# Hybrid DeltaNet and mLSTM layer: the step from 64-blocks to 128 in the inverse, all its products in pairs, with the last token block's matrices moved by transfers

## The chip, the cores and the metric

The kernel runs on one core of one Trainium2 chip. A core has five engines with instruction streams of their own: PE (TensorE, the matrix products), DVE (VectorE), ACT (ScalarE), POOL (GpSimd) and SP (SyncE, which here only issues transfers). Sixteen DMA engines carry the transfers that SP and ACT issue. The metric is the device time of one execution in microseconds.

## The reference

The layer takes 256 tokens of width 2048. From one wide projection of the normalized input come a gated DeltaNet with 32 value heads of 128 and an mLSTM with 8 heads; their outputs are projected, merged by gates and projected again. What the change touches is the DeltaNet's chunk algorithm, with chunks of 64 tokens:

```python
lower = jnp.where(strict, jnp.einsum('nbhid,nbhjd->nbhij', k_beta, kc) * decay, 0.0)
unit_lower = lower + jnp.eye(CHUNK, dtype=f32)
rhs = jnp.concatenate([v_beta, k_beta * jnp.exp(g_cum)[..., None]], axis=-1)
sol = lax.linalg.triangular_solve(unit_lower, rhs, left_side=True, lower=True, unit_diagonal=True)
...
def step(state, inp):
    attn_c, u_c, w_c, qd_c, kt_c, gt_c = inp
    v_new = u_c - jnp.einsum('bhck,bhkv->bhcv', w_c, state)
    o = jnp.einsum('bhck,bhkv->bhcv', qd_c, state) + jnp.einsum('bhij,bhjv->bhiv', attn_c, v_new)
```

The kernel doesn't carry a state from chunk to chunk. It treats 128 tokens as one block, inverts a unit triangular 128x128 matrix for each head and block, and applies it. The result is the same sequence.

## The kernel before

**The stream.** A planner (`Stream`) walks through all weight matrices in a fixed order. SP loads a piece of 1 MB into `raw` (line 169, a ring of three), ACT rounds it to `whi` (L173), DVE and at times POOL form the rest `wlo` (L174), and PE multiplies: projections with tokens on the output's rows are `pn` (L235), transposed ones are `pt` (L628 with `whi`, L632 with `wlo`). A piece is 1024 columns; PE does 12 products on it for `pn` and 16 pairs of high and low products for `pt`. The instruction order of each engine is the order in which the Python code calls it; no scheduler changes it.

**Side jobs.** After each used piece `side.step()` advances all side jobs, which are Python generators, by one `yield`. One step is thus one piece of projection work on PE. `wait(n)` lets n steps pass; `banks(n)` waits until n of the four PSUM slots for side jobs can be had; `side.debt` is an estimate of DVE time that other side jobs have yet to use, by which the block inverse on DVE is spread over steps (`side.room`).

**Periods.** The 32 heads are handled in eight periods, `zg` = 0 to 7, of two pairs each. In periods 0 to 5 the projection beside this work is mostly the DeltaNet's `pt`; in period 6 it is the mLSTM's `pn`, and in period 7 a `pt` of the mLSTM. A period has eight triangular 128x128 matrices: two blocks of 128 tokens for each of four heads, numbered m = 0 to 7; even m is a head's first 128 tokens, odd m its last. `au` holds the matrices, `um(m)` is the part of one that is inverted. The inverse grows from 32 to 64 to 128:

- `base_inverse` inverts the 32x32 diagonal blocks on DVE, in a packed form that SP moves through DRAM (`au` to `ud` to `ug`, then `xx` to `xd` to `xcmp`). `xcmp` and its transpose `ycmp` are copied to the diagonals of `x0` (128 rows, ACT) and `y0` (64 rows, DVE). `x0` becomes the inverse, `y0` the transpose of its first 64x64 block.
- `gdn_stage2` makes the off-diagonal 32x32 blocks with the products `mp` and `mx` and ACT's copies (L902 to `y0`, L905 to `x0`).
- The step from 64 to 128 needs, for every m, `mq` = the corner of `um(m)` times `y0` (first, L911: contracts rows 0 to 63, puts its output on rows 64 to 127) and `mz` = its copy `p2` times `x0` (second, L914: contracts rows 64 to 127, output on rows 0 to 63). As they use opposite corners of the array, an `mq` of one matrix and an `mz` of another can stand in a pair. Three blocks of instructions hold them: four `mq` of the even matrices; four `mq` of the odd ones with four `mz` of the even ones; and, behind the product `pa`, four `mz` of the odd ones.
- Then the inverse is applied: `pa` with the even inverses, `pb`, `pc` with the odd ones, and `po`.

**The waits around it.** `gdn_stage2` lets `wait(1 + (zg == 6))` steps pass between ACT's copies and the first `mq`, one step between the blocks, and two each ahead of `pb` and `pc`.

Of the kernel before, what the change touches and what calls it, by code (L numbers as in the profile page):

```python
# [7 lines left out]
F32 = mybir.dt.float32  # L8
F32R = mybir.dt.float32r
AF = mybir.ActivationFunctionType  # L10
# [5 lines left out]
P = 128  # L16
S = 256
# [101 lines left out]
def hybrid_layer_kernel(  # L119
# [25 lines left out]
    V, A, T, G, SP = nc.vector, nc.scalar, nc.tensor, nc.gpsimd, nc.sync  # L145
# [60 lines left out]
    def gtile(nm, held=False):  # L206
        i = slots[0] % 4
        slots[0] += 1
        t = pg.tile([P, 512], F32, name=nm, tag="g")
        freed[i] = 1 << 30 if held else side.t + 1  # L210
        slots[1][id(t)] = i, t
        return t

    def gfree(t):
        freed[slots[1].pop(id(t))[0]] = side.t

    def banks(n):

        while any(freed[(slots[0] + j) % 4] >= side.t for j in range(n)):
            yield  # L220
# [16 lines left out]
    side = Side()  # L237
    bp = x0 = y0 = None
# [209 lines left out]
    def branches_open():  # L448

        nonlocal bp, x0, y0  # L450
        side.drain()
        st.close()
        bp = br.enter_context(tc.tile_pool(name="bp", bufs=2))

        x0 = bp.tile([P, 8, P], F32, name="x0", tag="x0", bufs=1)
        y0 = bp.tile([64, 8, 64], F32, name="y0", tag="y0", bufs=1)
        G.memset(x0, 0.0)
        G.memset(y0, 0.0)

    def add_start_groups(bi):  # L460
# [12 lines left out]
        def after(g, ps):  # L473
            for b in range(2):
                if k0:
                    V.tensor_tensor(part[g][:, b], ps[b], part[g][:, b], op=ALU.add)  # L476
                elif bi or g in (0, 2, 3) or b == 0:
                    A.copy(part[g][:, b], ps[b])  # L478
                else:
                    V.tensor_copy(part[g][:, b], ps[b])  # L480
            if bi == len(BLOCKS) - 2 and g == 3:
                late_consts()
            if lastb:
                side.add(gate_values(g), 0)
                if g == NG - 1:
                    branches_open()
# [219 lines left out]
    def wait(n):  # L706
        for _ in range(n):
            yield
# [106 lines left out]
    def base_inverse(zg, res, zr):  # L815

        ud = res["ud"]
        xd = dr.tile([8, 4, 4, 8, 32], F32, name="xd", tag="xd", bufs=2)
        ug = bp.tile([P, 32, 32], F32, name="ug", tag="ug", bufs=1)
        for q in range(4):  # L820
            SP.dma_start(ug[32 * q:32 * q + 32],
                         ud[q].rearrange("m j i -> m (j i)").unsqueeze(0).broadcast_to([4, 8, 1024]))
        yield from wait(4)
        most = ROOM_US if zg else FIRST_ROOM_US
        yield from side.room(0.8, most)
        ugf = ug.rearrange("p j i -> p (j i)")
        V.memset(ugf[:, 0:1024:33], -1.0)
        nsu = bp.tile([P, 15], F32, name="nsu", tag="nsu", bufs=1)
        V.tensor_scalar(nsu, ugf[:, 34:34 + 66 * 15:66], -1.0, None, op0=ALU.mult)
        V.memset(ugf[:, 34:34 + 66 * 15:66], 0.0)  # L830
        xx = bp.tile([P, 8, 32], F32, name="xx", tag="xx", bufs=1)
        tmp = bp.tile([P, 8, 2, 32], F32, name="tmp", tag="tmp", bufs=1)
        V.tensor_copy(xx, eunit)
        for i in range(1, 32, 2):
            w = min(2, 32 - i)
            nq = (i + w - 2) // 4 + 1
            n = i + w
            us = 0.2 + 0.00105 * nq * w * n
            yield from side.room(us, most)
            V.tensor_tensor(tmp[:, 0:nq, 0:w, 0:n], xx[:, 0:nq, 0:n].unsqueeze(2).broadcast_to([P, nq, w, n]),  # L840
                            ug[:, 0:n, i:i + w].rearrange("p k c -> p c k").unsqueeze(1).broadcast_to([P, nq, w, n]),
                            op=ALU.mult)
            yield from side.room(us + 0.16 * (w - 1), most)
            V.tensor_reduce(xx[:, 0:nq, i:i + w], tmp[:, 0:nq, 0:w, 0:n], axis=AX.X, op=ALU.add, negate=True)
            if w == 2:
                V.scalar_tensor_tensor(xx[:, 0:nq, i + 1], xx[:, 0:nq, i], nsu[:, i // 2:i // 2 + 1],
                                       xx[:, 0:nq, i + 1], op0=ALU.mult, op1=ALU.add)
        yield from wait(1)
        SP.dma_start(xd.rearrange("qq q rg m i -> (q rg m) qq i"), xx)
        yield from wait(2 * (zg // 7))  # L850
        xcmp = bp.tile([P, 8, 32], F32, name="xcmp", tag="xcmp", bufs=1)
        for q in range(4):
            SP.dma_start(xcmp[32 * q:32 * q + 32], xd[:, q])
        yield from wait(5 - 2 * (zg // 7))
        side.debt += 1.1
        ycmp = bp.tile([P, 8, 32], F32, name="ycmp", tag="ycmp", bufs=1)
        V.transpose(ycmp.rearrange("p m i -> p (m i)"), xcmp.rearrange("p m i -> p (m i)"))
        for q in range(4):
            c = slice(32 * q, 32 * q + 32)
            A.copy(x0[c, :, c], xcmp[c])  # L860
            if q < 2:
                V.tensor_copy(y0[c, :, c], ycmp[c])
        res.update(xcmp=xcmp, ycmp=ycmp)
        yield
        while zg < 7 and side.t < res["t"] + STAGE2_STEPS - 1:
            yield
        side.add(gdn_stage2(zg, res, zr), 0)

    def gdn_stage2(zg, res, zr):

        au, xc, yc = [res["au", z] for z in range(2)], res["xcmp"], res["ycmp"]

        def um(m):
            return au[m // 4][:, m % 4 // 2, 256 + 384 * (m % 2):384 + 384 * (m % 2)]
# [8 lines left out]
        for m in range(8):  # L883
            for t in range(2):
                r, o = 64 * t, 64 * t + 32
                T.matmul(pss[t][o:o + 32, m * 32:(m + 1) * 32], um(m)[r:r + 32, o:o + 32], yc[r:r + 32, m],
                         start=True, stop=True)
        for t in range(2):
            o = 64 * t + 32
# [6 lines left out]
        for m in range(8):  # L896
            T.matmul(psx[0][32:64, S + m * 32:S + (m + 1) * 32], xc[32:64, m], pc_[32:64, m], start=True, stop=True)
            for t in (1, 0):
                r, o = 64 * t, 64 * t + 32
                T.matmul(psx[t][r:r + 32, m * 32:(m + 1) * 32], pc_[o:o + 32, m], xc[o:o + 32, m],  # L900
                         start=True, stop=True)
        A.activation(y0[32:64, :, 0:32], cols32(psx[0], S)[32:64], AF.Copy, scale=-1.0)  # L902
        for t in range(2):
            r = 64 * t
            A.activation(x0[r:r + 32, :, r + 32:r + 64], cols32(psx[t])[r:r + 32], AF.Copy, scale=-1.0)  # L905
            gfree(psx[t])
        yield from wait(1 + (zg == 6))
        p2 = bp.tile([P, 8, 64], F32, name="p2", tag="p2", bufs=1)

        def first(ps, j, m):  # L910
            T.matmul(ps[64:128, j * 64:(j + 1) * 64], um(m)[0:64, 64:128], y0[:, m], start=True, stop=True)  # L911

        def second(ps, j, m):
            T.matmul(ps[0:64, j * 64:(j + 1) * 64], p2[64:128, m], x0[64:128, m, 64:128], start=True, stop=True)  # L914

        def part64(ps, r, o):
            return ps[r:r + 64, o:o + S].rearrange("p (m i) -> p m i", m=4)

        yield from banks(1)
        psp = gtile("mq", True)  # L920
        side.debt -= 0.5
        for j in range(4):
            first(psp, j, 2 * j)
        A.activation(p2[64:128, 0:8:2], part64(psp, 64, 0), AF.Copy, scale=-1.0)
        yield
        yield from banks(1)
        psz = gtile("mz", True)
        side.debt -= 0.5
        for j in range(4):
            first(psp, 4 + j, 2 * j + 1)  # L930
            second(psz, j, 2 * j)
        A.copy(x0[0:64, 0:8:2, 64:128], part64(psz, 0, 0))
        A.activation(p2[64:128, 1:8:2], part64(psp, 64, S), AF.Copy, scale=-1.0)
        gfree(psp)
        yield

        rr = res["rr"].rearrange("p b z (h d) -> p b (z h d)", h=2)
# [1 line left out]
        heads = [(g, g // 2, g % 2, slice(g * P, (g + 1) * P)) for g in range(4)]  # L939
        yield from banks(1)  # L940
        pa = gtile("pa", True)
        side.debt -= 1.3
        for g, z, h, c in heads:
            T.matmul(pa[:, c], x0[:, 2 * g], rr[:, 0, c], start=True, stop=True)
        for j in range(4):
            second(psz, 4 + j, 2 * j + 1)
        A.copy(ys[:, 0], pa)
        gfree(pa)
        A.copy(x0[0:64, 1:8:2, 64:128], part64(psz, 0, S))
        gfree(psz)  # L950
        yield from wait(2)
        yield from banks(1)
        pb = gtile("pb", True)
# [42 lines left out]
        yield  # L996
        while "sz" not in zr:
            yield
        yield from wait(2)
        sz = zr["sz"]  # L1000
        for g, z, h, c in heads:
            if g == 2:
# [20 lines left out]
    def period_tail(zg, ps, qs, pr, res, zr):  # L1023
        yield from gdn_stage1(2 * zg + 1, ps, qs, pr, res)
        yield
        side.add(base_inverse(zg, res, zr), 2)
# [510 lines left out]
```

## Time and profile before

| | us |
|---|---|
| median of 3 runs | 1582.64 |
| lowest and highest run | 1582.38, 1582.78 |
| profiled execution, its own time | 1583.33 |
| its span, first to last instruction | 1581.6 |
| mean granted PE clock | 0.998 of full speed |

The profiled execution is 0.69 us above the median and 1.73 us longer than its span. In the page's rows a group stands as line, engine, operation, output<-input and count; `PE mq L911 x8` are eight passes of the four 64x64 products, since an f32 product shows two. All 64x64 products together are 256 passes:

```profile
L911 PE MATMUL mq<-y,au 64*64 64x64 f32 x128 | 10.8, 224 | 0.0
L914 PE MATMUL mz<-x,p 64*64 64x64 f32 x128 | 10.8, 224 | 0.0
```

The figures are busy time in us (passes that run side by side count once), mean ns of one, and idle time ahead of the group. A row of the chain of waits has a start, a length and what ran. A row of windows has the stretch, its length, the busy time and number of instructions of PE, PEld, DVE, ACT and POOL, the granted clock, the DMA engines' busy share and GB/s.

### The profile page before, as it was taken

Reading aid. Unit: us, or ns where it says so; the run is one execution under the profiler, and the core shown is the slowest. Engines: PE = TensorE matmul, PEld = TensorE weight load, DVE = VectorE, ACT = ScalarE, POOL = GpSimd, SP = SyncE. Lnnn points to the kernel's source line nnn. Section 1 sums busy time; section 2 is a strip of 40 time slices with the busy share of each in tenths; the row PEclk is TensorE's granted clock in tenths of the full one; section 3 lists DMA queues with packets and bytes.
Section 4 is the critical chain, followed back from the end, with each engine's and each line's share of the span. In section 5 each row is a group of like instructions: output and inputs, shape, how many; then the busy total and the mean of one; then the engine's idle time right before and its main releaser. Section 6 shows DMA issues by size and latency. Waiting matters only on the chain.

```text
span 1581.6 us, 23140 instructions
## 1 busy us (share of the span) xinstructions
PE 1565.7 (99%) x8574; PEld 1315.6 (83%) x8574; DVE 1159.7 (73%) x1884; ACT 967.2 (61%) x1608; POOL 249.7 (16%) x204
## 2 busy tenths in 40 slices
PE   8999999999999999999999999999999999999997
PEld 5888888888888888888888888888888888888886
DVE  6785556865789887988887988775868766756654
ACT  7754446765666676767676776766666554544443
POOL 4787761000000000000000000000000000100100
PEclk9999999999999999999999999999999999999999
DMA  9998775975565646575656565647878878766572
GB/s 379 392 385 334 267 288 188 288 245 193 182 195 175 209 147 202 167 201 168 202 167 198 172 199 171 199 142 247 281 270 314 339 264 298 282 237 237 213 269 107
DMA packets 167739, 372.22 MB, mean 235 GB/s; under 512 B 26021, under 2 KB 127797, under 8 KB 140105
## 3 DMA queue, kind: packets, MB, share of 16 engines
q1 hardware_dynamic: 167240, 370.13, 67.6%
q8 instruction: 67, 1.10, 0.3%
q10 hardware_dynamic: 290, 0.53, 0.1%
q14 instruction: 46, 0.38, 0.1%
q0 software_dynamic: 96, 0.09, 0.0%
HBM read 354.40 MB, written 16.31 MB: 234 GB/s over the span
## 4 chain that ended last, share of the span: by engine, by line
PE 81%; issue 13%; ACT 2%; DMA 1%; DVE 1%; POOL 1%; DVEq 0%; SPq 0%; ACTq 0%; POOLq 0%
PE pn L235 36%; PE pt L628 19%; PE pt L632 9%; PE py L235 8%; POOL mg L1327 1%; ACT whi L173 1%; DMA ya<-o_dr 1%; PE psa L235 1%; PE mq L911 1%; PE csil L305 0%; PE po L977 0%; PE pc L966 0%; PE po L976 0%; PE po L974 0%; PE pb L956 0%
## 5 line engine op out<-in xcount | busy, mean ns | idle before, releaser
L174 DVE TENSOR_TENSOR wlo<-raw,whi 128x1024 fp32r<-128x1024 f32 x453 | 556.1, 1235 | 241.1 <-ACT whi L173 240.2
L173 ACT CAST whi<-raw 128x1024 fp32r<-128x1024 f32 x516 | 532.1, 1046 | 261.3 <-PE pn L235 133.2
L235 PE MATMUL pn<-whi,h 128*128 128x512 f32 x1792 | 563.7, 392 | 0.9 <-ACT part L478 0.6
L628 PE MATMUL pt<-h,whi 128*128 128x512 f32 x1280 | 408.5, 400 | 0.0
L235 PEld LDWEIGHTS pn<-whi,h 128*128 128x128 f32 x1792 | 336.4, 188 | 71.9 <-ACT part L478 1.5
L235 PE MATMUL pn<-wlo,h 128*128 128x512 f32 x896 | 349.1, 390 | 0.9 <-POOL wlo L174 0.9
L632 PEld LDWEIGHTS pt<-h,wlo 128*128 128x128 f32 x1280 | 240.4, 188 | 56.6
L632 PE MATMUL pt<-h,wlo 128*128 128x256 f32 x1280 | 252.1, 278 | 0.0
L235 PEld LDWEIGHTS pn<-wlo,h 128*128 128x128 f32 x896 | 168.4, 188 | 35.4 <-POOL wlo L174 1.7
L628 PEld LDWEIGHTS pt<-h,whi 128*128 128x128 f32 x1280 | 195.4, 189 | 2.4
L174 POOL TENSOR_TENSOR wlo<-raw,whi 128x1024 fp32r<-128x1024 f32 (+1 forms) x63 | 145.7, 2320 | 51.6 <-ACT whi L173 51.6
L235 PE MATMUL py<-whi,yhi 128*128 128x512 f32 x384 | 150.8, 393 | 0.0
L235 PE MATMUL py<-whi,ylo 128*128 128x512 f32 x384 | 149.7, 390 | 0.0
L235 PE MATMUL py<-wlo,yhi 128*128 128x512 f32 x384 | 149.4, 389 | 0.0
L173 ACT CAST yhi<-ya 128x512 fp32r<-128x512 f32 x48 | 29.9, 622 | 130.3 <-PE py L235 114.9
L476 DVE TENSOR_TENSOR part<-pn,part 128x512 f32<-128x512 f32 x112 | 73.7, 685 | 45.2 <-PE pn L235 45.0
L719 POOL TENSOR_SCALAR_AFFINE_SELECT dd<-gb 128x256 f32<-128x256 f32 x40 | 25.9, 668 | 422.8 <-DMA gb<-rows 330.3
L174 DVE TENSOR_TENSOR ylo<-ya,yhi 128x512 fp32r<-128x512 f32 x48 | 33.2, 691 | 74.9 <-ACT yhi L173 72.2
L235 PEld LDWEIGHTS py<-whi,yhi 128*128 128x128 f32 x384 | 72.1, 188 | 15.6 <-ACT vt L1144 0.4
L235 PEld LDWEIGHTS py<-whi,ylo 128*128 128x128 f32 x384 | 72.1, 188 | 15.1
L235 PEld LDWEIGHTS py<-wlo,yhi 128*128 128x128 f32 x384 | 72.1, 188 | 14.9
L686 DVE SCALAR_TENSOR_TENSOR qs<-ab,gcv,qs 128x255 f32<-128x255 f32 (+2 forms) x192 | 81.0, 477 | 0.0
(263 smaller groups left out, 1612.9 us busy)
## 6 DMA issues: line engine op xcount, KB each, us to landing
raw<-in_dram SPq DMA_DIRECT2D x259, 1024.0 KB
ar<-in_dram SPq DMA_DIRECT2D x31, 1024.0 KB
raw<-in_dram SPq DMA_DIRECT2D x16, 512.0 KB
ya<-o_dr SPq DMA_DIRECT2D x32, 256.0 KB
gate_dr<-part SPq DMA_DIRECT2D x11, 512.0 KB
gb<-rows SPq DMA_DIRECT2D x20, 256.0 KB
raw<-in_dram SPq DMA_DIRECT2D x6, 768.0 KB
ug<-ud SPq DMA_DIRECT2D x32, 128.0 KB
```

The costliest lines, as they stand in the source:

```text
L173: A.copy(hi, src)
L174: (eng or V).tensor_tensor(lo, src, hi.bitcast(F32), op=ALU.subtract)
L235: T.matmul(ps, l, r, start=start and i == 0, stop=stop and i == 2, skip_group_check=True)
L476: V.tensor_tensor(part[g][:, b], ps[b], part[g][:, b], op=ALU.add)
L628: T.matmul(ps, hi[:, o:o + P], h2[:, k].rearrange("p a s -> p (a s)"), start=k == 0, stop=k == KC - 1, skip_group_check=True)
L632: T.matmul(ps[:, 0:S], lo[:, o:o + P], h_hi[:, k], start=False, stop=k == KC - 1, skip_group_check=True)
L686: V.scalar_tensor_tensor(dst[:, n, sh:], ab[i][:, 0:S - sh], taps(n, 3 - sh), dst[:, n, sh:], op0=ALU.mult, op1=ALU.add)
L719: G.affine_select(dd[:, :, blk * S:blk * S + P], gb[:, :, blk * P:(blk + 1) * P], pattern=[[0, 2], [1, P]], compare_op=ALU.is_ge, fill=-1e ...
L911: T.matmul(ps[64:128, j * 64:(j + 1) * 64], um(m)[0:64, 64:128], y0[:, m], start=True, stop=True)
L1327: G.tensor_tensor(mcols(b, hf, cg), mcols(b, hf, cg), s_, op=ALU.add)
```

## The change

The lower triangle of the odd matrices (the last 128 tokens' block of each head) is moved to the opposite corner, so that the odd matrix of a head and its even one are multiplied in a pair, for `mq` and for `mz` alike. `y0` gets 128 rows. SP loads the odd corners of `um` into rows 64 to 127 of `y0`'s even columns (two transfers a period, behind `xcmp`); ACT issues a transfer that copies `y0`'s odd columns from rows 0 to 63 to rows 64 to 127, one that moves the odd matrices' lower diagonal block of `x0` into `p2`, and, behind the second block, one that brings the odd result from `p2` back into `x0`. The two blocks of products hold eight each, in pairs. The count of products is the same. The first block comes a step later in periods 0 to 5 and 7 and where it was in period 6; the estimates `side.debt` change with it.

```diff
-        y0 = bp.tile([64, 8, 64], F32, name="y0", tag="y0", bufs=1)
+        y0 = bp.tile([P, 8, 64], F32, name="y0", tag="y0", bufs=1)
...
             SP.dma_start(xcmp[32 * q:32 * q + 32], xd[:, q])
+        for z in range(2):
+            SP.dma_start(y0[64:128, 4 * z:4 * z + 4:2], res["au", z][0:64, :, 704:768])
...
-        yield from wait(1 + (zg == 6))
         p2 = bp.tile([P, 8, 64], F32, name="p2", tag="p2", bufs=1)
-        def first(ps, j, m):
-            T.matmul(ps[64:128, j * 64:(j + 1) * 64], um(m)[0:64, 64:128], y0[:, m], start=True, stop=True)
-        def second(ps, j, m):
-            T.matmul(ps[0:64, j * 64:(j + 1) * 64], p2[64:128, m], x0[64:128, m, 64:128], start=True, stop=True)
...
-        for j in range(4):
-            first(psp, j, 2 * j)
-        A.activation(p2[64:128, 0:8:2], part64(psp, 64, 0), AF.Copy, scale=-1.0)
-        yield
...
-        for j in range(4):
-            first(psp, 4 + j, 2 * j + 1)
-            second(psz, j, 2 * j)
-        A.copy(x0[0:64, 0:8:2, 64:128], part64(psz, 0, 0))
-        A.activation(p2[64:128, 1:8:2], part64(psp, 64, S), AF.Copy, scale=-1.0)
+        ev, od = slice(0, 8, 2), slice(1, 8, 2)
+        A.dma_start(y0[64:128, od], y0[0:64, od])
+        A.dma_start(p2[0:64, ev], x0[64:128, od, 64:128])
...
+        def corners(nm, low, high):
+
+            ps = [gtile(nm, True) for _ in range(2)]
+            side.debt -= 1.0
+            for j in range(4):
+                for p_, r, (l, x_) in ((ps[0], 0, low(2 * j)), (ps[1], 64, high(2 * j))):
+                    T.matmul(p_[64 - r:128 - r, j * 64:(j + 1) * 64], l, x_, start=True, stop=True)
+            return part64(ps[0], 64), part64(ps[1], 0), ps
+
+        yield from wait(2)
+        yield from banks(2)
+        pe, po_, ps = corners("mq", lambda m: (um(m)[0:64, 64:128], y0[0:64, m]),
+                              lambda m: (y0[64:128, m], y0[64:128, m + 1]))
+        A.activation(p2[64:128, ev], pe, AF.Copy, scale=-1.0)
+        A.activation(p2[0:64, od], po_, AF.Copy, scale=-1.0)
...
+        yield
+        yield from banks(2)
+        po_, pe, ps = corners("mz", lambda m: (p2[0:64, m + 1], p2[0:64, m]),
+                              lambda m: (p2[64:128, m], x0[64:128, m, 64:128]))
+        A.copy(x0[0:64, ev, 64:128], pe)
+        A.copy(p2[64:128, od], po_)
+        A.dma_start(x0[0:64, od, 64:128], p2[64:128, od])
...
-        side.debt -= 1.3
+        side.debt -= 0.8
...
-        for j in range(4):
-            second(psz, 4 + j, 2 * j + 1)
...
-        A.copy(x0[0:64, 1:8:2, 64:128], part64(psz, 0, S))
...
-        yield from wait(2)
+        yield from wait(2 - zg // 7)
```

On PE in period 0, the third block of before is what follows `pa` in the first place; the rows end with the next projection piece:

```order
L628 MATMUL pt_4600<-h_87,whi 128x512
L628 MATMUL pt_4601<-h_87,whi 128x512
L632 MATMUL pt_4600<-h_87,wlo 128x256
L632 MATMUL pt_4601<-h_87,wlo 128x256
L944 MATMUL pa<-rr,x_2797 128x128 x4
L914 MATMUL mz<-x_2797,p_4678 64x64 x4
L628 MATMUL pt_4795<-h_87,whi 128x512
```

In the changed kernel the place of `pa` in the same period, one step later and beside the next matrices' `psa` products, reads:

```order
L632 MATMUL pt_4795<-h_87,wlo 128x256
L632 MATMUL pt_4796<-h_87,wlo 128x256
L952 MATMUL pa<-rr,x_2797 128x128 x4
L235 MATMUL psa<-qh 128x512
L235 MATMUL psa<-ql,qh 128x512
```

The four `mz` behind `pa` are gone; they stand in the second block, between `mz` of the even matrices (`x_2797` is `x0`, `y_2798` is `y0`, `p_...` is `p2`).

On ACT in period 6, around the copies that follow `mx`, before (L902 and L905 are the copies, L924 the one that follows the first `mq`):

```order
L902 ACTIVATE y_2798<-mx_9977 32x8x32
L905 ACTIVATE x_2797<-mx_9977 32x8x32
L905 ACTIVATE x_2797<-mx_9978 32x8x32
L727 ACT_TABLE_LOAD
L727 ACTIVATE dd<-dd,tt 128x128
```

and in the changed kernel:

```order
L904 ACTIVATE y_2798<-mx_10021 32x8x32
L907 ACTIVATE x_2797<-mx_10021 32x8x32
L907 ACTIVATE x_2797<-mx_10022 32x8x32
L911 DMA y_2798<-y_2798 64x4x64
L912 DMA p_10050<-x_2797 64x4x64
L727 ACT_TABLE_LOAD
L727 ACTIVATE dd<-dd,tt 128x128
```

Two issues of transfers have come between the copies and what followed them.

On DVE in period 6, where the 32x32 blocks' transposes are made, before (`wlo` is the stream's work, `ycmp` and `y` the period's):

```order
L686 SCALAR_TENSOR_TENSOR qs<-ab,mcv,qs 128x253 x2
L174 TENSOR_TENSOR wlo<-raw,whi 128x1024 x2
L857 STREAM_TRANSPOSE ycmp<-xcmp 128x256
L862 COPY y_2798<-ycmp 32x8x32 x2
L174 TENSOR_TENSOR wlo<-raw,whi 128x1024 x4
L827 MEMSET ug 128x32
```

and in the changed kernel:

```order
L686 SCALAR_TENSOR_TENSOR qs<-ab,mcv,qs 128x253 x2
L859 STREAM_TRANSPOSE ycmp<-xcmp 128x256
L864 COPY y_2798<-ycmp 32x8x32 x2
L174 TENSOR_TENSOR wlo<-raw,whi 128x1024 x6
L827 MEMSET ug 128x32
```

The transpose and the two copies have moved ahead of two pieces of `wlo`.

More of the change, by code (lines that the diff above doesn't have):

```diff
@@ L906, in gdn_stage2 @@
             gfree(psx[t])
-        yield from wait(1 + (zg == 6))
         p2 = bp.tile([P, 8, 64], F32, name="p2", tag="p2", bufs=1)
-        def first(ps, j, m):
-            T.matmul(ps[64:128, j * 64:(j + 1) * 64], um(m)[0:64, 64:128], y0[:, m], start=True, stop=True)
-        def second(ps, j, m):
-            T.matmul(ps[0:64, j * 64:(j + 1) * 64], p2[64:128, m], x0[64:128, m, 64:128], start=True, stop=True)
-        def part64(ps, r, o):
-            return ps[r:r + 64, o:o + S].rearrange("p (m i) -> p m i", m=4)
@@ L919, in gdn_stage2 @@
-        yield from banks(1)
-        psp = gtile("mq", True)
-        side.debt -= 0.5
-        for j in range(4):
-            first(psp, j, 2 * j)
-        A.activation(p2[64:128, 0:8:2], part64(psp, 64, 0), AF.Copy, scale=-1.0)
-        yield
-        yield from banks(1)
-        psz = gtile("mz", True)
-        side.debt -= 0.5
-        for j in range(4):
-            first(psp, 4 + j, 2 * j + 1)
-            second(psz, j, 2 * j)
-        A.copy(x0[0:64, 0:8:2, 64:128], part64(psz, 0, 0))
@@ L933, in gdn_stage2, with part64 @@
-        A.activation(p2[64:128, 1:8:2], part64(psp, 64, S), AF.Copy, scale=-1.0)
-        gfree(psp)
+        ev, od = slice(0, 8, 2), slice(1, 8, 2)
+        A.dma_start(y0[64:128, od], y0[0:64, od])
+        A.dma_start(p2[0:64, ev], x0[64:128, od, 64:128])
+        def part64(ps, r):
+            return ps[r:r + 64, 0:S].rearrange("p (m i) -> p m i", m=4)
+        def corners(nm, low, high):
[5 more added lines that the diff above has]
+            return part64(ps[0], 64), part64(ps[1], 0), ps
@@ new lines, in gdn_stage2 @@
+        yield from wait(2)
[4 more added lines that the diff above has]
+        A.activation(p2[0:64, od], po_, AF.Copy, scale=-1.0)
+        for p_ in ps:
+            gfree(p_)
+        yield
+        yield from banks(2)
+        po_, pe, ps = corners("mz", lambda m: (p2[0:64, m + 1], p2[0:64, m]),
+                              lambda m: (p2[64:128, m], x0[64:128, m, 64:128]))
@@ L935, in gdn_stage2 @@
+        A.copy(x0[0:64, ev, 64:128], pe)
+        A.copy(p2[64:128, od], po_)
+        A.dma_start(x0[0:64, od, 64:128], p2[64:128, od])
+        for p_ in ps:
+            gfree(p_)
         yield
@@ L941, in gdn_stage2 @@
         pa = gtile("pa", True)
-        side.debt -= 1.3
+        side.debt -= 0.8
         for g, z, h, c in heads:
             T.matmul(pa[:, c], x0[:, 2 * g], rr[:, 0, c], start=True, stop=True)
-        for j in range(4):
-            second(psz, 4 + j, 2 * j + 1)
         A.copy(ys[:, 0], pa)
         gfree(pa)
-        A.copy(x0[0:64, 1:8:2, 64:128], part64(psz, 0, S))
-        gfree(psz)
         yield from wait(2)
```

## The prediction

> **What bounds the kernel now.** I read the page's first part (busy time of each engine), its fourth (the chain that ended last), then the waits of PE, then two stretches of 80 us.
>
> ```profile
> span 1581.6 us, 23140 instructions
> PE 1565.7 (99%) x8574; PEld 1315.6 (83%) x8574; DVE 1159.7 (73%) x1884; ACT 967.2 (61%) x1608; POOL 249.7 (16%) x204
> ...
> PE 81%; issue 13%; ACT 2%; DMA 1%; DVE 1%; POOL 1%; DVEq 0%; SPq 0%; ACTq 0%; POOLq 0%
> ...
> PE csil L305 <- ACT ar L303: 4.5, 1, 4.5
> PE mpt L1127 <- ACT oT L1019: 1.0, 1, 1.0
> ...
> 600.00:680.00 80.00, 80.00 (x545) 69.20 (x544) 68.42 (x146) 56.50 (x112) 6.36 (x9) 1.00 0.59 181
> 1000.00:1080.00 80.00, 78.97 (x595) 66.25 (x594) 54.90 (x108) 53.01 (x108) 2.65 (x2) 1.00 0.61 199
> ```
>
> PE is busy for 1565.7 of 1581.6 us and carries the chain. Its two longest single waits are 4.5 us at the start and 1.0 us. In a whole gated-delta period (600 to 680) it never stops. So PE work that goes is time that goes, one for one, as long as nothing else is late; and a transfer that comes late is time lost, one for one. That is the whole question here.
>
> **The change part by part.** *The block that goes.* Before, each period has three places with 64x64 products: four `mq`, then four `mq` with four `mz`, then four `mz` behind `pa`. The chain of waits in the first period, where every row starts where the row before ends:
>
> ```profile
> 527.65 0.60 PE mq L911 x8
> 528.25 0.66 PE pt L628 x2
> ...
> 531.03 0.23 PE pt L632 x2
> ...
> 531.87 0.66 PE pt L628 x2
> ...
> 532.76 0.47 PE pt L628 x2
> ...
> 534.86 0.89 PE pa L944 x8
> 535.75 0.60 PE mz L914 x8
> 536.36 0.66 PE pt L628 x2
> ...
> 543.84 0.89 PE pb L956 x8
> 544.73 0.46 PE pt L628 x2
> ```
>
> Eight passes alone take 0.60 us. The middle block runs from 531.26 (531.03 + 0.23) to 531.87: 0.61 us for sixteen passes, as the pairs in opposite corners run together. Behind each of the three blocks the next `pt` pair takes 0.66 in place of 0.46 to 0.47, which is 0.20 more; behind `pb`, of full 128x128 products, it takes 0.46. So a block costs 0.80 us however full it is. The changed kernel has two blocks of sixteen and nothing behind `pa`. **One block of 0.80 us less in each of eight periods is 6.4 us.** Period 6, in the mLSTM part, shows the same price with other neighbours:
>
> ```profile
> 1005.47 5.66 PE pn L235 x24
> 1011.13 0.60 PE mq L911 x8
> 1011.73 2.95 PE pn L235 x12
> ...
> 1015.29 2.95 PE pn L235 x12
> 1018.24 0.89 PE pa L944 x8
> 1019.13 0.60 PE mz L914 x8
> 1019.74 5.67 PE pn L235 x24
> ```
>
> Twelve `pn` products behind a block take 2.95, twenty-four take 5.67, so the second dozen takes 2.72 and the block's surcharge is 0.23. The middle block takes 0.61 again (1014.68 to 1015.29).
>
> *The transfers that come.* For each period ACT issues one transfer into `y0` and one into `p2` right behind its `x<-mx` copies; the first block needs the former, the second the latter. ACT issues a third, into `x0`, for products (`pc`) that come several steps later; I cost its landing at nothing. What is needed are the moments at which ACT is done with `x<-mx`, and prices of transfers:
>
> ```profile
> 525.12 0.76 ACT L905 ACTIVATE x<-mx 32x256 f32<-32x256 f32 x2
> ...
> 1006.18 0.76 ACT L905 ACTIVATE x<-mx 32x256 f32<-32x256 f32 x2
> 1010.02 1.98 ACT L173 CAST whi<-raw 128x1024 fp32r<-128x1024 f32 x2
> 1015.09 1.05 ACT L173 CAST whi<-raw 128x1024 fp32r<-128x1024 f32 x1 [2.69 <-DMA raw<-in_dram]
> ...
> 1068.32 0.78 ACT L905 ACTIVATE x<-mx 32x256 f32<-32x256 f32 x2
> ...
> 1070.82 0.60 PE mq L911 x8
> ...
> 0.75 0.52 ACTq L292 DMA_DIRECT2D ar<-in_dram  x1
> 3.35 2.00 ACT L303 ACTIVATE ar<-ar 1x1024 f32<-1x1024 f32 x2 [0.76 <-DMA ar<-in_dram]
> ...
> SPq L853 <- DMA xd<-xx: 34.4, 7, 5.1
> ...
> 1003.27 0.35 SPq L169 DMA_DIRECT2D raw<-in_dram  x1
> ...
> 606.00:610.00 4.00, 4.00 (x28) 3.43 (x27) 1.23 (x1) 2.50 (x4) 0.00 (x0) 1.00 1.09 268
> 1007.00:1011.00 4.00, 4.00 (x19) 3.08 (x17) 0.01 (x1) 3.99 (x9) 0.00 (x0) 1.00 1.02 240
> ```
>
> Cover in periods 0 to 5: ACT is done at 525.88, and the new first block stands one step later than the old, a step being 2.79 us of `pt` (528.25 to 531.03, and a little): 527.65 + 2.79 = 530.44, so 4.5 us. The second block, one step and one block further (531.87 - 528.25 = 3.6), gives `p2` 8.2 us. In period 6 the step is not moved: 1006.94 to 1011.13 is 4.2 us, and `p2` has till 1014.68, 7.7 us. In period 7 ACT is done at 1069.10 and the block moves one step from 1070.82, 4.5 us.
>
> What a transfer of this size takes there, no row shows. The nearest small one that ACT issues, 8 KB at the start, is there 2.6 us after its issue begins (0.75 to 3.35). The nearest on the slow side for periods 0 to 5 is `xd`, in many small pieces: SP waits for it 34.4 us in 7 times, 4.9 in the mean, with an issue of some 0.5 before it, 5.4. The two window rows show that the DMA engines are full just then (share 1.09 and 1.02): a weight load, `ug` and `gb` are under way. I take `y0` (64 rows x 4 heads x 256 B, 256 pieces, 16 to each of 16 DMA engines) to go piece by piece in turn with SP's loads. In periods 0 to 5 these come in pieces of 1 KB: at 268 GB/s over 16 engines one takes 0.06 us, so 16 turns add 1.0 us, and `y0` lands 3.6 us behind ACT, `p2` 1.0 later and its issue of 0.52: **hidden, 0** (bounds: 0, and 0.9 a period by the `xd` row, 5.4 - 4.5). Period 7 I cost the same.
>
> Period 6 loads weights in 8 KB rows. At 240 GB/s one piece is 0.55 us, and 16 turns are 8.7 us if there are raw pieces to take turns with. There are: the load issued at 1003.27 lands only at 1015.09, where ACT waits 2.69 us for it. The ends are thus no wait (2.6 us, by the row at the start) and 11.8 us, by this load's own row: 1006.94 + 11.8 = 1018.8, 7.6 late. By turns, `y0` lands between 1009.6 and 1015.7. I take the middle, 1012.7 to 1013.3 with the issue, and 2.2 us of waiting before the first block; `p2`, behind it, is through when the loads ahead are, and costs some 0.4 more. **Period 6: minus 2.6.**
>
> [...]
>
> *Steps that move on DVE.* In period 6 `ycmp` and two `y` copies go ahead of two `wlo` pieces, by the order of DVE's instructions:
>
> ```profile
> 996.84 2.35 DVE L174 TENSOR_TENSOR wlo<-raw,whi 128x1024 fp32r<-128x1024 f32 x2
> 999.11 0.43 DVE L857 STREAM_TRANSPOSE ycmp<-xcmp 128x256 f32<-128x256 f32 x1
> 999.57 0.58 DVE L862 COPY y<-ycmp 32x256 f32<-32x256 f32 x2
> ...
> 998.62 0.39 PE L235 MATMUL pn<-wlo,h 128*128 128x512 f32 x1
> ```
>
> The first of the two `wlo` ends half way, near 998.05, and PE takes it at 998.62: 0.57 us of margin. The three that go ahead of it take 1.04 (999.11 to 1000.15). **Minus 0.5.** In periods 1 to 5 the same step and parts of the block inverse come earlier too, with DVE busy for 68.42 of 80 us; margins of a few tenths are left in places. I take 0, with 0 and 1.0 a period (the 1.04 without a margin) as ends.
>
> *The rest at nothing.* ACT: three issues of 0.52 a period, 1.6 us of its 23.5 idle (80 - 56.50). Two of them push the casts of 1010.02 by a microsecond; the `pn` that come after 1011.73 use such pieces, and DVE, which works between, is idle there (0.01 busy from 1007 to 1011). Without that cover the 1.0 us would be PE's. [...] SP: two loads into `y0`, and in period 6 `gb` and a weight load behind them; PE waits for no weight load in the list of waits, and three are held in the ring. POOL is 16% busy and its `gb` work comes early. PE: in periods 0 to 5 `pa`, `pb` and `pc` stand a step later, `po` where it stood; DVE's use of `pb` then follows later, among the pieces weighed above. PSUM: the blocks ask for two banks at once, and in the order of PE's instructions the blocks stand where they are reckoned here.
>
> **Sum.** 6.4 - 2.6 - 0.5 = 3.3 us less than the profiled execution's 1583.33: 1580.0. That execution is 0.69 above the median of the runs, 1582.64, so the median should be **1579.3**.
>
> **The rivals.** *Hidden everywhere.* `y0` lands inside 4.2 us in period 6 too. For it: the 2.6 us of the row at the start, 64 KB being little beside 240 GB/s (0.3 us). Against it: DMA share 1.02, and loads of 11.8 us. Then 6.4 - 0.5 (or - 0): 1576.7 (1576.2). [...]
>
> *DVE is late in periods 1 to 5.* Some tenths to 1.0 us in some of them: 1 to 3 us of the gain go back, 1580.5 to 1582.6, and it reads as no change. For it: 68.42 of 80 us busy. Against it: PE never waits for DVE there now.
>
> *Transfers are late in every period: slower.* The mechanism is the queue in front of the first block: `y0` shares the engines with `ug`, `gb` and a weight load. With the longest `xd` row, 5.1 and an issue of 0.6, it lands 5.7 us behind ACT, 1.2 too late, in seven periods 8.4; with 3.1 in period 6 that is 11.5 against 6.4, and the median is 1587.7. It is slower by over 0.2% from a wait of 0.9 us a period (6.4 + 3.2 - 3.1 over seven), which is a landing 5.4 us behind ACT; the gain is gone from 0.5. For it: the shares of 1.09. Against it: pieces there are 1 KB or less.
>
> *The pairs don't run together.* Two products that are both fed from `y0` would then take 1.2 us and not 0.61 a block: the saving is gone, 1583. Against it stands the old middle block of 0.61.
>
> **Chances and range.** A gain or loss under 0.2%, 3.2 us, can't be told from no change here. Forecast (1578.0 to 1581.0) 0.41, half of it beyond 1579.5; hidden everywhere 0.34; DVE late 0.13; transfers late everywhere 0.09; pairs apart 0.03. Faster: 0.34 + 0.20 = 0.54; slower: 0.09; the rest, 0.37, same. The range goes from all hidden, 1575.8, to the DVE rival's end, 1582.8.
>
> **What would show it.** Two 64x64 blocks a period of 0.61 with one `pt` pair of 0.66 behind each, and none behind `pa`, show the saving; a period from first block to first block should be 0.8 shorter. In period 6 PE should wait for a DMA into `y` before `mq`, 2 us or so, and at most shortly for `p` before `mz`; a `pn` should wait 0.5 for `wlo` near 998. A PE wait for `y` in periods 0 to 5 would make the forecast wrong on the slow side, none in period 6 on the fast side.

## The result: slower by 1.3%

The changed kernel takes 1603.34 us (median of 4 runs, 1601.97 to 1605.61) against 1582.60 before: ratio 1.0133, 95% interval 1.0115 to 1.0150. The prediction was 1579.3 with a range to 1582.8; the result lies 20.5 us above its upper end. The profiled execution took 1603.37, its span 1601.6, 20.0 more than before, at a granted clock of 0.992 in place of 0.998.

The page of the changed kernel, its first part:

```profile
span 1601.6 us, 23247 instructions
PE 1567.5 (98%) x8574; PEld 1317.1 (82%) x8574; DVE 1161.6 (73%) x1884; ACT 966.8 (60%) x1608; POOL 247.5 (15%) x204
```

and PE's waits (us in total, times, longest):

```profile
PE mq L923 <- DMA y<-y: 11.2, 6, 2.4
PE mq L923 <- issue: 7.8, 1, 7.8
```

Two things stand there. PE waits 19.0 us at the first block, 11.2 in periods 0 to 5 and 7.8 in period 6 (called "issue" as nothing in the profile is named as what came last). And its busy time has *risen*, from 1565.7 to 1567.5, though a block a period is gone. The chain of waits in the first period shows the former:

```profile
524.65 7.87 DMA y<-y
532.52 0.14 issue
532.66 0.65 PE mq L923 x14
533.30 0.66 PE pt L628 x2
...
536.28 0.61 PE mz L923 x16
536.89 0.66 PE pt L628 x2
...
539.89 0.89 PE pa L952 x8
540.78 0.70 PE psa L235 x3
```

The blocks are as foreseen: 0.61 for sixteen passes, 0.65 for the fourteen of `mq` that follow the wait (the first two, which read only `y0`'s lower rows, run before it), 0.66 for the `pt` pair behind, none behind `pa`. But the transfer into `y0` takes 7.87 us from its issue to its landing, and PE stands still for the last 2.4 of them. The same view in period 5 shows the latter:

```profile
933.33 7.71 DMA y<-y
941.04 0.14 issue
941.18 1.08 PE mq L923 x14
942.26 1.15 PE pt L628 x2
943.41 0.43 PE pt L632 x2
...
947.66 0.61 PE mz L923 x16
```

After a gap of 2.3 us the fourteen passes take 1.08 in place of 0.65, the `pt` pair 1.15 in place of 0.66, and the next 0.43 in place of 0.23, all at about half speed, for some 6 us. In windows that begin where a gap ends (the fourth goes on from the third), the granted clock, the third figure from the end, reads:

```profile
694.86:697.86 3.00, 3.00 (x27) 2.62 (x28) 2.69 (x11) 1.70 (x3) 0.00 (x0) 1.00 0.87 285
775.97:778.97 3.00, 3.00 (x22) 2.57 (x23) 2.69 (x11) 1.69 (x3) 0.74 (x2) 0.65 0.85 275
941.18:944.18 3.00, 3.00 (x20) 2.59 (x21) 2.65 (x12) 1.69 (x3) 0.00 (x0) 0.50 0.64 193
944.18:947.18 3.00, 3.00 (x11) 2.52 (x10) 2.83 (x8) 0.00 (x0) 1.03 (x3) 0.50 0.76 258
1031.57:1034.57 3.00, 3.00 (x19) 2.50 (x20) 0.42 (x2) 1.69 (x3) 0.00 (x0) 0.50 0.44 183
```

Three of the seven gaps, in periods 3, 5 and 6, are followed by a stretch of half clock; the one that ends at 694.86, 1.6 us long, is not, though the one in period 3 (at 775.97) is shorter, 1.5 us.

### The profile page after: what moved, and what is told of

It reads as the page before. It is cut to its first block, busy times and chain, and to the rows that moved or that the text cites. A ratio compares the mean times of both kernels' runs of the same rounds, so it can differ in the third digit from the quotient of the medians.

```text
span 1601.6 us, 23247 instructions
## 1 busy us (share of the span) xinstructions
PE 1567.5 (98%) x8574; PEld 1317.1 (82%) x8574; DVE 1161.6 (73%) x1884; ACT 966.8 (60%) x1608; POOL 247.5 (15%) x204
## 4 chain that ended last, share of the span: by engine, by line
PE 48%; issue 13%; DMA 3%; POOL 1%; DVE 1%; ACT 1%; DVEq 0%; POOLq 0%; ACTq 0%
PE pn L235 15%; PE pt L628 13%; PE py L235 8%; PE pt L632 6%; DMA y<-y 3%; POOL mg L1331 1%; PE psa L235 1%; PE po L980 0%; PE po L978 0%; PE pc L970 0%; PE po L981 0%; PE pb L960 0%; PE pa L952 0%; PE mq L923 0%; PE pt L1020 0%
## 5 line engine op out<-in xcount | busy, mean ns | idle before, releaser
L719 POOL TENSOR_SCALAR_AFFINE_SELECT dd<-gb 128x256 f32<-128x256 f32 x40 | 21.3, 555 | 423.6 <-DMA gb<-rows 291.5
```

Source lines behind the costliest of these rows:

```text
L719: G.affine_select(dd[:, :, blk * S:blk * S + P], gb[:, :, blk * P:(blk + 1) * P], pattern=[[0, 2], [1, P]], compare_op=ALU.is_ge, fill=-1e ...
```

## The experiments

Theory A: `y0`'s transfer stands behind what SP's loads have already put to the DMA engines; PE waits for it, and the gap brings the clock down. Rival B: the pairs themselves cost the clock. Rival C: the transfer is slow because its many small pieces take turns one by one with the loads, as I had reckoned.

**The pairs without the transfers.** ACT's three transfers are taken out; the odd matrices' corners are left out of the result.

```diff
-        A.dma_start(y0[64:128, od], y0[0:64, od])
-        A.dma_start(p2[0:64, ev], x0[64:128, od, 64:128])
+        G.memset(p2[0:64, ev], 0.0)
...
-        A.dma_start(x0[0:64, od, 64:128], p2[64:128, od])
```

> The changed kernel without ACT's three transfers (p2's lower rows are set to zero on POOL, y0's odd columns in the upper rows stay zero, x0's odd corner is not brought back: the odd matrices' corner is left out of the result); steps, pairs and positions as in the changed kernel. Theory A: PE waits for no transfer, 1576 to 1577.5 us, clock 0.998. Theory B: pairs are still there, so 1583 to 1586 us and the lower clock. If the transfers also hold up weight loads, this is faster than the run with more cover by that much; I expect less than 1 us.

1578.54 us, ratio 0.9971 (0.9961 to 0.9981), clock 0.998. Its busy times:

```profile
PE 1560.5 (99%) x8574; PEld 1310.8 (83%) x8574; DVE 1160.6 (74%) x1884; ACT 967.7 (61%) x1608; POOL 253.6 (16%) x212
```

PE's waits:

```profile
PE py L235 <- ACT vt L1146: 1.5, 1, 1.5
PE pc L968 <- DVE rr L961: 1.2, 1, 1.2
```

and `pa` in periods 0 and 1 of its chain of waits, with that of the kernel before in period 1 below:

```profile
537.23 0.89 PE pa L950 x8
...
616.59 0.89 PE pa L950 x8
```

```profile
615.00 0.89 PE pa L944 x8
```

A period is 79.36 us (537.23 to 616.59) in place of 80.14 (534.86 to 615.00): 0.78 less, where 0.80 was predicted. No half clock follows any block (the mean is 0.998, as before the change), so B falls: it isn't the pairs that bring the clock down. PE's busy time over the whole run is 5.2 us below the kernel before (1565.7 - 1560.5); eight times 0.78 would be 6.2, and where the other 1.0 stays no run here isolates. The time is 1.0 to 2.5 us above what I expected: besides that, two waits appear elsewhere (`pc` for DVE in period 6, `py` for ACT later), 2.7 us.

**A gap without the change.** The kernel before with its three blocks, and one 64 KB transfer on ACT's queue that the first `mq` needs.

```diff
-        yield from wait(1 + (zg == 6))
         p2 = bp.tile([P, 8, 64], F32, name="p2", tag="p2", bufs=1)
+        A.dma_start(p2[0:64, 0:8:2], y0[:, 0:8:2])
+        yield from wait(2 - zg // 7 + (zg == 6))
...
-            T.matmul(ps[64:128, j * 64:(j + 1) * 64], um(m)[0:64, 64:128], y0[:, m], start=True, stop=True)
+            T.matmul(ps[64:128, j * 64:(j + 1) * 64], um(m)[0:64, 64:128], (y0[:, m] if m % 2 else p2[0:64, m]), start=True, stop=True)
```

(with `STAGE2_STEPS` 31 and one step less ahead of `ycmp`, in periods 0 to 6, so that the chain up to `mx` runs a step earlier)

> The kernel before with its three blocks and no pairing of a head's two matrices, but with one ACT transfer (y0's even columns into free rows of p2, 64 KB) that the first mq needs, with a cover of two steps. Theory A: PE stands idle some 2 us in periods 0 to 5 and 3 to 6 us in periods 6 and 7, 15 to 22 us in all, and the clock falls behind the gaps, another 4 to 10 us: 1600 to 1614 us, clock under 0.996. Theory B: the idle time alone, clock 0.998: the time is 1582.6 plus the gaps, PE's busy time 1566 as before.

1621.47 us, ratio 1.0252 (1.0227 to 1.0278), clock 0.990. PE's waits:

```profile
PE mq L912 <- DMA p<-y: 25.6, 8, 3.9
```

its busy times:

```profile
PE 1577.6 (97%) x8574; PEld 1324.3 (82%) x8574; DVE 1163.3 (72%) x1884; ACT 968.0 (60%) x1608; POOL 248.8 (15%) x204
```

and the chain of waits and a window in period 1:

```profile
607.64 7.39 DMA p<-y
615.03 0.14 issue
615.17 0.65 PE mq L912 x8
```

```profile
615.17:618.17 3.00, 3.00 (x17) 2.65 (x18) 2.24 (x8) 1.42 (x2) 0.00 (x0) 0.69 0.60 196
```

No pair was added, and still 25.6 us of gaps come with 11.9 us of longer PE time (1577.6 - 1565.7): the clock falls because of the gap. Both are more than I had expected, and the time lies 7 us above its range. The transfer takes 7.39 us here too.

**Fewer, larger pieces.** `y0` is laid out with the odd matrices side by side, so that its transfer has 64 pieces of 1 KB and not 256 of 256 B.

```diff
-        y0 = bp.tile([P, 8, 64], F32, name="y0", tag="y0", bufs=1)
+        y0 = bp.tile([P, 2, 4, 64], F32, name="y0", tag="y0", bufs=1)
...
-        A.dma_start(y0[64:128, od], y0[0:64, od])
+        A.dma_start(y0[64:128, 1].rearrange("p j i -> p (j i)"), y0[0:64, 1].rearrange("p j i -> p (j i)"))
```

> The changed kernel with y0 laid out so that the transfer into its upper rows moves 64 pieces of 1 KB instead of 256 of 256 B (4 instead of 16 for each DMA engine), the same bytes. Theory C (my prediction's: pieces take turns one by one with the loads): a quarter of the turns, so y lands in periods 0 to 5 after 3 to 4 us in place of 6.8 to 7.9, no gap there, period 6 under 3 us: 1577 to 1584 us. Theory A2 (the transfer starts only when what SP's loads have already put ahead of it on an engine is through, and then goes in one run): y lands as late as in the changed kernel, 1599 to 1606 us.

1591.83 us, ratio 1.0058 (1.0043 to 1.0073), between the two ranges. PE's waits:

```profile
PE mq L923 <- DMA y<-y: 7.1, 6, 1.4
PE mq L923 <- issue: 4.1, 1, 4.1
```

and the transfer in the chain of waits in period 0:

```profile
525.09 6.82 DMA y<-y
```

A quarter of the pieces makes it 1.05 us faster in this period (7.87 to 6.82), 0.2 to 1.0 in the other five. By C it would have landed after 3 to 4 us, so C falls as the main cause in periods 0 to 5. In period 6, where the loads come in pieces of 8 KB, the gap falls from 7.8 us to 4.1, and in the two runs further down that leave its loads and its 256 pieces as they are it is 7.1 and 7.7. So the number of `y0`'s own pieces counts for nearly half there: neither C nor its opposite, that `y0` lands as late as before, holds in full. The gaps, now 1.4 us or less in periods 0 to 5, bring no half clock there (it reads 1.00 in the windows behind them), so that 7.8 us less of waiting (19.0 - 11.2) gained 11.5.

**Half the loads.** Half of each weight load of the `pt` pieces is left out, and those columns are made from the other half's data.

```diff
+            if bp is not None and len(s_.shape) == 3 and c == 0 and s_.shape[1] == 8 and s_.shape[2] == 256:
+                SP.dma_start(raw[:, 0:1024].rearrange("p (k n) -> p k n", k=4), s_[:, 0:4])
```

> The changed kernel with half of each weight load of the pt pieces left out (the second half of the columns is made from the first half's data), so that the DMA engines have little in hand when y's transfer is issued in periods 0 to 5; the loads of the pn pieces (period 6) are whole. If y waits for what SP's loads have ahead of it: it lands within 4.5 us there, no gap in periods 0 to 5, and period 6 keeps its gap of 7 to 8 us with a fall of the clock: 1584 to 1590 us. If something else holds y up (ACT's queue, its small pieces): still 6.5 us or more, gaps as before, 1598 us or above.

1586.62 us, ratio 1.0024 (1.0015 to 1.0033). The one wait left at the first block:

```profile
PE mq L931 <- issue: 7.1, 1, 7.1
```

The transfer's issue on the timeline of period 0, and the chain of waits there:

```profile
525.22 0.69 ACTq L919 DMA_DIRECT2D y<-y  x1
```

```profile
530.29 0.23 PE pt L640 x2
530.53 0.61 PE mq L931 x16
```

The transfer, unchanged in pieces, queue and place, is there within 5.3 us (525.22 to 530.53), and all six gaps are gone; only period 6, whose loads were left whole, keeps its gap. (Whether it lands within the 4.5 us that I expected, a chain without a wait doesn't show.) So it is the load on the DMA engines that holds `y0` up, 7.87 us in this period with the loads whole. That the columns are left out changes no step on PE.

**Half the loads in period 6 too.** The same for the loads that are issued from period 5's second stage to period 6's blocks.

```diff
+            if cut and len(s_.shape) == 2 and c == 0 and s_.shape[1] == 2048:
+                SP.dma_start(raw[:, 0:1024], s_[:, 0:1024])
```

> As the run with half loads for the pt pieces, but the pn pieces' loads ahead of and in period 6 are halved as well (half of their columns left out of the computation). If the backlog of SP's loads is the whole loss: period 6's gap falls from 7.1 to under 3 us, and the time to 1578 to 1582 us; with no gap and no half clock at all 1577. If period 6 waits for something else than the loads: its gap stays at 6 to 8 us and the time at 1585 to 1589.

PE's wait at the first block:

```profile
PE mq L938 <- DMA y<-y: 2.6, 1, 2.6
```

1582.22 us, ratio 0.9994 (0.9984 to 1.0004), above the 1578 to 1582 I had expected by a little; its profiled execution took 1579.11. Period 6's gap falls from 7.1 to 2.6 us: the same cause. In the profiled execution no half clock follows the 2.6 us (1.00 in the 6 us behind them); whether it does in the longer ones, and makes their 2 to 6 us, no profile of them shows.

**Loads in two halves.** The same bytes, each `pt` load as two transfers.

```diff
+                for q in range(2):
+                    SP.dma_start(raw[:, 1024 * q:1024 * q + 1024].rearrange("p (k n) -> p k n", k=4),
+                                 s_[:, 4 * q:4 * q + 4])
```

> The changed kernel with each weight load of the pt pieces issued as two transfers of half the size, the same bytes. If an engine changes to y's queue after the load that it is at (a turn is one transfer), y lands 1 us or more sooner in periods 0 to 5, and their 11.2 us of gaps fall below 6: 1588 to 1598 us. If all that SP has issued before goes first, or pieces take turns, nothing changes in y: 1599 to 1606 us.

1603.84 us, ratio 1.0136 (1.0121 to 1.0150), as the changed kernel. In its chain of waits, period 2:

```profile
688.70 6.93 DMA y<-y
```

The changed kernel took 7.04 there. So the size of SP's transfers, halved with the same bytes and pieces, made no difference.

**The transfers in SP's queue.** `y0`'s and `p2`'s first transfers are issued by SP.

```diff
-        A.dma_start(y0[64:128, od], y0[0:64, od])
-        A.dma_start(p2[0:64, ev], x0[64:128, od, 64:128])
+        SP.dma_start(y0[64:128, od], y0[0:64, od])
+        SP.dma_start(p2[0:64, ev], x0[64:128, od, 64:128])
```

> The changed kernel with y's and p's transfers issued by SP, at the same place of the program, behind its own weight loads in one queue. If ACT's queue gives y no turn ahead of the loads that are already issued (y is served in order of arrival), y lands as late as in the changed kernel, 6.5 to 8 us behind ACT's copies and 12 to 14 in period 6: 1599 to 1608 us. If the second queue did give it turns between the loads' pieces, the time in SP's queue is longer: over 9 us to land in periods 0 to 5, 1612 us or above.

1633.76 us, ratio 1.0322 (1.0307 to 1.0338). PE's waits, and the transfer in the chain of waits of period 1:

```profile
PE mq L923 <- DMA y<-y: 34.1, 6, 8.8
PE mq L923 <- issue: 6.2, 1, 6.2
```

```profile
612.84 9.98 DMA y<-y
```

The figures of the second expectation came, 9.0 to 10.8 us in periods 1 to 5 and over 1612 us, but the timelines of that period, here and in the changed kernel, say that turns between the loads' pieces are not the main reason:

```profile
612.84 3.15 SPq L911 DMA_DIRECT2D y<-y  x1
```

```profile
606.73 0.60 ACTq L911 DMA_DIRECT2D y<-y  x1
```

SP's issue, right behind that of a weight load, takes 1.7 to 3.7 us in periods 1 to 5, ACT's 0.6. Counted from the end of the issue, `y0` lands after 6.7 to 7.3 us from SP's queue and after 6.1 to 7.1 from ACT's. So ACT's queue spares `y0` the long issue; once issued, it is held up nearly as long in either queue. Which piece an engine takes next is left open.

**More cover.** The chain up to `mx` starts a step earlier, the first block stays, and in period 6 it comes two steps later.

```diff
-STAGE2_STEPS = 32
+STAGE2_STEPS = 31
...
-        yield from wait(5 - 2 * (zg // 7))
+        yield from wait(4 - (zg // 7))
...
-        yield from wait(2)
+        yield from wait(2 + (zg < 7)+2*(zg==6))
...
-        yield from wait(2)
+        yield from wait(2 - (zg==6))
...
-        yield from wait(2 - zg // 7)
+        yield from wait(2 - zg // 7-(zg==6))
```

> The changed kernel with more steps between the transfers and the first block: the chain up to mx starts one step earlier, the first block of periods 0 to 5 stays where it is, that of period 6 comes two steps later and pb, pc and the end take fewer steps. Theory A (PE lost 19.0 us waiting for y, and some 8 us more because the granted clock falls after such gaps): no gap before mq, clock 0.998 again, the 6.4 us of the missing block show, 1575.5 to 1577.5 us. Theory B (pairs of 64x64 products in every block lower the clock or make PE slower): no gap, but PE's busy time stays near 1567 us and the clock near 0.993, 1583 to 1586 us.

1585.24 us, ratio 1.0016 (1.0006 to 1.0025): the gain was not there. PE's waits:

```profile
PE pc L970 <- DVE rr L963: 3.7, 1, 3.7
PE mq L923 <- issue: 2.1, 3, 1.0
PE mq L923 <- DMA y<-y: 0.5, 1, 0.5
```

Nearly all waits for `y0` went, but my shorter distances in period 6 (the edit `wait(2 - (zg==6))`, made ahead of `pb` and of `pc`) put `pc` before DVE was ready for it: a new gap of 3.7 us, and a half clock behind it (0.50 in the 3 us from its end). PE's busy time is 1563.4, 2.9 above the run without transfers.

**Cover and large pieces together**, with the distances ahead of `pb` and `pc` back at 2 and a step more for period 7:

```diff
-        yield from wait(2)
+        yield from wait(3 + 2 * (zg == 6))
...
-        yield from wait(2 - zg // 7)
+        yield from wait(2 - (zg // 6) - (zg == 6))
```

> The run with more cover again, with y0 in the layout of 1 KB pieces, one step more in period 7 and without the steps that were taken out ahead of pb and pc in period 6 (there pc waited 3.7 us for DVE). If gaps and the clock behind them are all that the changed kernel loses: no gap of over 0.5 us in the eight periods, no half clock, and the 0.78 us a period that the run without transfers showed: 1576 to 1578.5 us, faster than before by 0.25 to 0.4%. If the transfers cost something besides (weight loads held up, ACT's queue), it stays at 1580 or above.

**1578.59 us, ratio 0.9974 (0.9964 to 0.9983)**: faster than both kernels. PE's waits, and a piece of the chain of waits in period 6:

```profile
PE pc L970 <- DVE rr L963: 0.8, 1, 0.8
PE pn L235 <- DVE wlo L174: 0.4, 1, 0.4
```

```profile
1032.02 1.23 DVE wlo L174
1033.25 0.61 DVE rr L963
1033.90 1.16 PE pc L970 x8
```

No wait for `y0` is left and the clock is 0.999. The two waits for DVE in period 6, 1.2 us, are what goes back there. The time is just above the upper end of what I expected, and the same as without transfers, with PE busy for 1561.0 us against 1560.5: hidden transfers cost about a microsecond at most (that run had 2.7 us of waits of its own).

## Why the prediction was wrong, point by point

- **The block that goes** (6.4 us): right in mechanism and near in size. The run without transfers has 0.78 us less in each of periods 0 to 5; its PE time over the whole run is 5.2 us lower.
- **"`y0` lands 3.6 us behind ACT ... hidden, 0"**: this is the step that failed. It landed after 6.75 to 7.87 us in periods 0 to 5. I had started from a transfer of 2.6 us at the kernel's start, where the DMA share over it is 0.52, and let the pieces take turns one by one, 1.0 us more: an estimate, and no run shows such turns. With the loads halved it landed in under 5.3, with a quarter of the pieces in no less than 6.4: in these periods the time goes by what is ahead, and the number of its own pieces is a small part (0.2 to 1.05 us). I had the share of 1.09 in front of me and the `xd` row of 5.4 to 5.7, and treated that row as the far end of the range; it was nearer than the row I took, and still too low.
- **Period 6, minus 2.6**: right that the longest wait is there, behind loads in 8 KB pieces (with these loads halved the gap is 2.6, with a quarter of `y0`'s pieces 4.1); the size was off: 7.8. The 2.2 in it came from turns of 0.55 us a piece, an estimate that no run shows. `p2` made no wait.
- **The price of a gap.** "A transfer that comes late is time lost, one for one" was wrong too. Gaps of 19.0 us came with 7.0 us of slower PE work (busy 1567.5 against 1560.5 in the run without transfers), and the granted clock alone accounts for that: in the windows behind the three gaps it takes 1.7, 3.2 and 2.3 us. The account: 1581.6 - 5.2 + 19.0 + 7.0 = 1602.4 against a span of 1601.6; PE's other waits are 0.8 shorter. No row before could show it, as PE hardly ever stopped for over a microsecond, but it belonged in the range as an unknown.
- **DVE's steps, minus 0.5 in period 6**: not seen. The run without transfers has the same steps and no gap ahead of them, and its list of waits has none for DVE's `wlo`; 0.4 us shows only in the two runs with more cover, where the chain starts a step earlier. "DVE is late in periods 1 to 5" did not happen: periods of 79.36 throughout.
- **The rival on the slower side** named this mechanism and priced it at 1587.7: 11.5 us of waits where there were 19.0, and no clock. Its chance of 0.09 was too low, since it rested on the nearest row on the slow side and on the two rows that showed full DMA engines.
- **Ends without a working**: "all hidden, 1575.8" is 1576.2 by the rival's own sum, and "DVE late", 1 to 3 us above 1579.3, is 1580.3 to 1582.3, not 1580.5 to 1582.6 or 1582.8. The result lies far from both.

## What to carry to other kernels

A small transfer that is put between two steps took here, in the main, the time of what the DMA engines had in hand when it was issued, not its own: the 64 KB of `y0` 6.75 to 7.87 us in periods 0 to 5, where the DMA share over it is 0.88 to 1.13, and under 5.3 with the loads halved, against 2.6 for the 8 KB at the start, at a share of 0.52. Take its price from a row that lands under the same share, and give it a cover of that and a step more. Where the loads came in large pieces, fewer pieces of its own helped too (in period 6 the gap fell from 7.8 us to 4.1). On a kernel that PE bounds, price a gap on PE at its length and, where it may bring the half clock, 1.6 to 3.2 us more, as measured here; over all gaps of a run this came to 1.4 to 1.5 times their length (26.0 for 19.0 us, 37.5 for 25.6). A step moved for cover must be checked against the engine that delivers to the step behind it: here two distances shortened by a step brought a wait of 3.7 us and a half clock behind it (0.50 for 3 us).

## What the runs showed of the hardware that was not expected

The granted clock fell to 0.50 for 3 to 6 us after a short gap of PE. Over the profiles of the changed kernel and of the experiments, but for the first 16 us, of which there is no clock record, it followed every gap of 3.1 us or more (eighteen) and none of 1.4 us or less; between 1.5 and 2.8 us it followed four gaps of fifteen (1.5, 2.1, 2.3 and 2.6 us), and not others of 1.6, 2.1, 2.4, 2.6 and 2.8. By the clock records of the changed kernel's trace the three stretches behind gaps are 3.41, 6.83 and 10.24 us long and begin at 776.84, 940.68 and 1026.02, the first 0.87 us behind its gap and the other two within theirs; in the run with a gap without the change the window from 955.94 (0.79 over 3 us) puts the begin of one about 1.7 us behind its gap. By the windows behind the gaps, a stretch cost PE 1.6 to 3.2 us. Why gaps of like length differ in this, and what sets the length of a stretch, no run shows.
